# A convolution's product and gate turned by VectorE and DMA instead of TensorE, with the gate products moved to the end of the projection

## The chip, the cores and the metric

The kernel runs on one core of a Trainium2 chip. The metric is the device time of one execution, in microseconds. TensorE (PE) multiplies matrices, VectorE (DVE) and ScalarE (ACT) work on vectors, GpSimd (POOL) does small things, and SyncE (SP) issues most of the DMA transfers. Each engine works through its own list of instructions in order and waits for the others by semaphores.

## The reference

A decoder trunk of four layers over 256 tokens of 1024 numbers, all float32. Each layer adds half a SwiGLU feed-forward (2816 wide), then a mixer, then another half SwiGLU, each on an RMS-normalised x. The mixers by layer are: short gated convolution, latent attention, spatial gating, and short gated convolution again. The change touches the convolution (layers 0 and 3) and the spatial gating (layer 2):

```python
def short_conv_mixer(x, w_in, conv_k, w_out):
    proj = x @ w_in
    b_gate, c_gate, h = proj[..., :d], proj[..., d:2 * d], proj[..., 2 * d:]
    z = c_gate * h
    conv = lax.conv_general_dilated(z, conv_k[:, None, :], ...)   # 3 taps, causal, per channel
    return (b_gate * conv) @ w_out

def spatial_gating_mixer(x, w_in, v_norm, w_s, b_s, w_out):
    z = jax.nn.gelu(x @ w_in)
    u, v = z[..., :SG_WIDTH], z[..., SG_WIDTH:]
    v = rms_norm(v, v_norm)
    ...
    return (u * mixed.reshape(bsz, s, SG_WIDTH)) @ w_out
```

## The kernel before

**Products.** The 256 tokens are two tiles of 128, and each weight serves both. To keep float32 accuracy a weight is split into a rounded part `whi` (ScalarE, L106) and a remainder `wlo` (VectorE, L113), and the left operand likewise; a product is then three matmuls (L299, L300, L302): rounded by rounded, rounded by remainder, remainder by rounded. A unit of weights is 128 x 1024 numbers (two rows of the contraction at width 512), so a unit is six matmuls of 128 x 512. Units are split up to three ahead of their use, from six raw buffers that SyncE loads (L93), and nine buffers of split units go round.

**The order.** The order is written out by the program's own loop: two generators, one for each token tile, take turns, and one turn emits the products of one unit (six matmuls). The first tile runs four of its steps ahead. What is to follow a product some turns later is put in a list (`later(turns, ...)`) and emitted when its turn comes, on whatever engines it needs. A unit's remainder is emitted on VectorE at the start of the next turn.

**Turning.** A result has tokens on partitions; as the left operand of the next product it must have channels there. There are two ways. `transposed` lets TensorE transpose four 128 x 128 blocks into PSUM (L261). The other way is a VectorE transpose within blocks of 32 x 32, a DMA write of the half to DRAM and four DMA reads back that put the blocks in place; the feed-forward's hidden half takes this way always (`turned`), and x does in most places (`prepare_x`, L415 to L431), where SyncE's weight loads are held back from the write until the reads.

**The convolution block** (`conv`, lines 512 to 560). The projection makes c, h and b, each in two halves of 512 channels. A group of the first three products shares the first half of x, which is ready earlier (`linear_group`); in the kernel before these are c, h and b of half 0, and then c, h and b of half 1 follow. When an h is done, VectorE makes z = c*h (L548), two turns later TensorE transposes it, ScalarE copies it out of PSUM (L523), and VectorE applies three taps to each of four blocks (L528, L530). When a b is done ScalarE takes it out of PSUM (L553), TensorE transposes it, VectorE multiplies the gate (L537), and the result is split (L253, L254) as the left operand of the output product. The output product `rows_into_x` takes rows 0 to 3 (half 0) first and rows 4 to 7 (half 1) after.

**The spatial block** (`spatial`): v of both halves and u of half 0 in the group, then u of half 1. The product m = u * mixed (L639) is transposed by TensorE and split.

## Time and profile before

| what | value |
|---|---|
| median of 3 runs | 1857.88 us (1857.31 to 1858.77) |
| the profiled execution's own time | 1856.6 us |
| its span (first to last instruction) | 1854.9 us |
| TensorE busy | 1833.3 us, 99% |
| VectorE busy | 1119.6 us, 60% |
| ScalarE busy | 913.9 us, 49% |
| DMA | 400.26 MB, 216 GB/s on average |

Busy time of TensorE counts a stretch in which matmuls follow without a hole, so 99% says how seldom it waits and not how fast it works. A timeline row gives the start, the duration, the engine, the line, the operation, what it writes and reads, and in square brackets how long its engine was idle before it and who ended that.

### The profile page before, as it was taken

The numbers are of one execution on the slowest core, as the hardware profiler recorded it, in microseconds if no ns is written. First come the engines' busy times: TensorE is split into PE (matmuls) and PEld (weight loads), VectorE is DVE, ScalarE is ACT, GpSimd is POOL, SyncE is SP. The second block draws the span as 40 slices with busy tenths as digits, with TensorE's granted clock in tenths as the row PEclk, the third lists the DMA queues.
The fourth block names the chain that finished last, engine by engine and source line by source line (L and its number), as shares of the span: only waits on it lengthen the run. The fifth ranks groups of instructions, "written<-read, shape, count | busy, mean of one in ns | idle before, by whom it ended". The sixth has DMA issues, their size and how long they took to land.

```text
span 1854.9 us, 23375 instructions
## 1 busy us (share of the span) xinstructions
PE 1833.3 (99%) x8518; PEld 1506.0 (81%) x8518; DVE 1119.6 (60%) x1357; ACT 913.9 (49%) x1300; POOL 103.9 (6%) x222
## 2 busy tenths in 40 slices
PE   8999999999999989999999999999999999999999
PEld 6888878888888878888888888888888888788887
DVE  5655676655665576666556555665645665775662
ACT  5443645443644376544454446554545454545451
POOL 1000000000501031000010001000000000000000
PEclk9999999999999999999999999999999999999999
DMA  7776657776777550687777766577857785657782
GB/s 265 241 240 218 209 179 216 240 241 210 235 244 238 193 160 15 201 259 232 221 238 256 228 220 216 175 232 234 264 185 243 242 261 178 213 181 235 233 269 75
DMA packets 228980, 400.26 MB, mean 216 GB/s; under 512 B 17126, under 2 KB 77696, under 8 KB 228864
## 3 DMA queue, kind: packets, MB, share of 16 engines
q1 hardware_dynamic: 227856, 397.08, 67.0%
q8 instruction: 66, 1.08, 0.2%
q0 software_dynamic: 608, 1.11, 0.2%
q10 hardware_dynamic: 400, 0.57, 0.1%
q14 instruction: 50, 0.41, 0.1%
HBM read 365.67 MB, written 33.03 MB: 215 GB/s over the span
## 4 chain that ended last, share of the span: by engine, by line
PE 96%; ACT 2%; DVE 2%; issue 0%; DMA 0%; DVEq 0%; ACTq 0%
PE acc L299 31%; PE acc L300 31%; PE acc L302 31%; PE tr L261 1%; PE acc L938 1%; PE acc L911 1%; ACT whi L106 1%; DVE wlo L113 0%; DVE s L530 0%; ACT s L836 0%; ACT s L253 0%; PE acc L620 0%; DMA s<-in_norm_g_dram 0%; ACT s L817 0%; ACT s L860 0%
## 5 line engine op out<-in xcount | busy, mean ns | idle before, releaser
L299 PE MATMUL acc<-whi,s 128*128 128x512 f32 (+1 forms) x2664 | 1025.2, 385 | 2.8 <-ACT whi L106 1.3
L300 PE MATMUL acc<-wlo,s 128*128 128x512 f32 (+1 forms) x2664 | 1019.8, 383 | 2.1 <-DVE wlo L113 2.1
L302 PE MATMUL acc<-whi,s 128*128 128x512 f32 (+1 forms) x2664 | 988.2, 383 | 0.0
L113 DVE TENSOR_TENSOR wlo<-raw,whi 128x1024 fp32r<-128x1024 f32 (+1 forms) x634 | 747.3, 1212 | 131.0 <-ACT whi L106 129.2
L106 ACT ACTIVATE whi<-raw 128x1024 fp32r<-128x1024 f32 (+1 forms) x634 | 636.6, 1047 | 138.9 <-PE acc L302 120.3
L299 PEld LDWEIGHTS acc<-whi,s 128*128 128x128 f32 x2664 | 500.9, 188 | 107.8 <-ACT whi L106 2.5
L300 PEld LDWEIGHTS acc<-wlo,s 128*128 128x128 f32 x2664 | 501.0, 188 | 106.0 <-DVE wlo L113 3.0
L302 PEld LDWEIGHTS acc<-whi,s 128*128 128x128 f32 x2664 | 500.7, 188 | 106.1 <-DVE s L254 0.7
L479 ACT ACTIVATE s<-acc,rstd 128x512 f32<-128x512 f32 (+1 forms) x96 | 62.6, 652 | 446.4 <-PE acc L302 440.4
L487 DVE SCALAR_TENSOR_TENSOR s<-acc,rstd,s 128x512 f32<-128x512 f32 (+1 forms) x96 | 67.7, 705 | 173.6 <-PE acc L302 171.8
L286 DVE TENSOR_TENSOR s<-big,s 128x512 fp32r<-128x512 f32 x96 | 61.8, 644 | 128.1 <-ACT s L285 127.9
L381 ACT ACTIVATE s<-x 128x512 bf16<-128x512 f32 x48 | 30.2, 630 | 163.6 <-DVE x L400 125.9
L254 DVE TENSOR_TENSOR s<-s,s 128x512 fp32r<-128x512 f32 (+1 forms) x58 | 39.9, 688 | 107.6 <-ACT s L253 107.6
L389 POOL TENSOR_TENSOR total<-ss,ss 128x1 f32<-128x1 f32 x26 | 14.8, 570 | 1417.1 <-ACT s L381 1417.1
L400 DVE SCALAR_TENSOR_TENSOR x<-acc,x 128x512 f32<-128x512 f32 x32 | 22.1, 692 | 117.3 <-PE acc L302 117.2
L285 ACT ACTIVATE s<-big 128x512 fp32r<-128x512 f32 x96 | 56.3, 586 | 22.1 <-DMA big<-turn 22.0
L489 DVE STREAM_TRANSPOSE big<-s 128x512 f32<-128x512 f32 (+1 forms) x96 | 64.1, 667 | 3.3
L253 ACT ACTIVATE s<-s 128x512 fp32r<-128x512 f32 (+1 forms) x58 | 36.5, 629 | 42.1 <-DVE s L537 21.6
L431 ACT ACTIVATE s<-s,columns 128x128 f32<-128x128 f32 x136 | 43.1, 388 | 1.9 <-DMA s<-xturn 1.7
L261 PE MATMUL tr<-ident,s 128*128 128x128 f32 (+1 forms) x222 | 33.3, 276 | 9.8 <-DVE s L781 5.1
L261 PEld LDWEIGHTS tr<-ident,s 128*128 128x128 f32 (+1 forms) x222 | 25.8, 138 | 17.9 <-DVE s L781 7.3
L415 DVE STREAM_TRANSPOSE s<-x 128x512 f32<-128x512 f32 x34 | 24.2, 711 | 1.2
(123 smaller groups left out, 410.6 us busy)
## 6 DMA issues: line engine op xcount, KB each, us to landing
raw<-in_ffn_gate_dram SPq DMA_DIRECT2D x176, 512.0 KB, 4.8
raw<-in_ffn_up_dram SPq DMA_DIRECT2D x176, 512.0 KB, 5.0
raw<-in_ffn_down_dram SPq DMA_DIRECT2D x176, 512.0 KB, 5.0
raw<-in_conv_w_in_dram SPq DMA_DIRECT2D x48, 512.0 KB, 4.7
turn<-big SPq DMA_DIRECT2D x32, 512.0 KB, 4.0
big<-turn SPq DMA_DIRECT2D x128, 128.0 KB, 4.4
xturn<-s SPq DMA_DIRECT2D x34, 256.0 KB, 4.2
s<-xturn SPq DMA_DIRECT2D x136, 64.0 KB, 2.0
```

Of the source, the lines that this page charges most:

```text
L106: nc.scalar.activation(hi, src, AF.Copy)
L113: self.nc.vector.tensor_tensor(out=lo, in0=src, in1=hi.bitcast(F32), op=ALU.subtract)
L261: nc.tensor.transpose(tr[: part.shape[-1], n, :], part, ident)
L285: nc.scalar.activation(hi.rearrange("p k (i b) -> p k i b", b=32), src, AF.Copy)
L286: nc.vector.tensor_tensor(out=lo.rearrange("p k (i b) -> p k i b", b=32), in0=src, in1=hi.bitcast(F32).rearrange("p k (i b) -> p k i b", b ...
L299: nc.tensor.matmul(ps, lhsT=ah[:, k, :], rhs=wh[:, wk, c], start=first, stop=False)
L300: nc.tensor.matmul(ps, lhsT=ah[:, k, :], rhs=wl[:, wk, c], start=False, stop=False)
L302: nc.tensor.matmul(ps, lhsT=al[:, k, :], rhs=wh[:, wk, c], start=False, stop=last)
L431: nc.scalar.activation(xg[:, k, :].rearrange("p (i b) -> p i b", b=32), y[:, :, k], AF.Copy, scale=g[:, k : k + 1])
L479: nc.scalar.activation(sg[n], ps[:, :w], AF.Silu, scale=r)
L487: nc.vector.scalar_tensor_tensor(out=h, in0=ps[:, :w], scalar=r, in1=sg[n], op0=ALU.mult, op1=ALU.mult)
L489: nc.vector.transpose(z[0][:, :, k0 : k0 + w // P].rearrange("p j k b -> p k j b"), h.rearrange("p (k j b) -> p k j b", j=4, b=32))
```

## The change

In the convolution block both z (c*h) and b now go the other way: `turn_half`, taken out of `prepare_x`, transposes in blocks on VectorE, writes, reads, and calls what follows eight turns later (`M_TAKE`). The taps read a copy that ScalarE makes in four pieces (L529); the gate multiplies what was read (L542). The order of the six products is changed to c0, h0, c1, then h1, b0, b1, so both gates come last, just ahead of the output product. In the spatial block the half 1 of m goes this way, and half 0 still through TensorE. The DRAM buffers for such turns become eight.

```diff
-X_TURN, X_WRITE, X_READ, X_TAKE = 2, 1, 3, 12
+X_TURN, X_WRITE, X_READ, X_TAKE, M_TAKE = 2, 1, 3, 12, 8
...
+    def turn_half(src, take, turns):
+
         z = slot([P, 4, 4, 32])
-        nc.vector.transpose(z.rearrange("p j k b -> p k j b"), x_half(t, h).rearrange("p (k j b) -> p k j b", j=4, b=32))
-        d = dram.tile([4, 32, 4, 4, 32], F32, tag="xturn", name=name("xturn"))
+        nc.vector.transpose(z.rearrange("p j k b -> p k j b"), src.rearrange("p (k j b) -> p k j b", j=4, b=32))
+        d = dram.tile([4, 32, 4, 4, 32], F32, tag="xturn", name=name("xturn"), bufs=8)
         y = slot([P, 4, 4, 32])
...
         later(X_WRITE, write)
         later(X_READ, read)
-        later(X_TAKE, take)
+        later(turns, lambda: take(y))
...
-        def convolved(j, z):
-            zp = transposed([z[:, k * P : (k + 1) * P] for k in range(4)])
+        def convolved(j, y):
...
-            nc.scalar.activation(zT[:, :, 2 : P + 2], zp, AF.Copy)
+            for k in range(4):
+                nc.scalar.activation(zT[:, k, 2 : P + 2].rearrange("p (i b) -> p i b", b=32), y[:, :, k], AF.Copy)
...
-        def gated(j, bs):
-            bT = transposed([bs[:, k * P : (k + 1) * P] for k in range(4)])
+        def gated(j, y):
             m = slot([P, 4, P])
-            nc.vector.tensor_tensor(out=m, in0=bT, in1=shared["cv", t, j], op=ALU.mult)
+            nc.vector.tensor_tensor(out=m.rearrange("p k (i b) -> p i k b", b=32), in0=y,
+                                    in1=shared["cv", t, j].rearrange("p k (i b) -> p i k b", b=32), op=ALU.mult)
...
-            later(3, lambda: convolved(j, z))
+            turn_half(z, lambda y: convolved(j, y), M_TAKE)
...
-            later(2, lambda: gated(j, bs))
-
-        yield from linear_group(t, a, 512, NK, [lambda ps, f=f: f(0, ps) for f in (c_done, h_done, b_done)])
-        for f in (c_done, h_done, b_done):
-            f(1, (yield from linear(t, a, 512, NK)))
+            turn_half(bs, lambda y: gated(j, y), M_TAKE)
+
+        yield from linear_group(t, a, 512, NK, [lambda ps: c_done(0, ps), lambda ps: h_done(0, ps), lambda ps: c_done(1, ps)])
+        for f, j in ((h_done, 1), (b_done, 0), (b_done, 1)):
+            f(j, (yield from linear(t, a, 512, NK)))
...
-            later(2, lambda: gated(j, m))
+            if j == 0:
+                later(2, lambda: gated_by_pe(j, m))
+            else:
+                turn_half(m, lambda y: gated(j, y), M_TAKE)
```

The lists of two engines change as follows in the first convolution block (layer 0). `wlo79` is the remainder of weight unit 79, `acc` a product's PSUM bank, `tr` a transposed one, `columns1` the taps, `raw` a weight buffer, `xturn` the DRAM buffer of a turn.

VectorE before, around the first gate: the last taps of the first tile, two splits, the gate (L537) and the remainder of its result, and the second tile's c*h (L548).

```order
L530 SCALAR_TENSOR_TENSOR s_232_1946<-s_231_1943,columns1_85,s_232_1946 128x128 x2
L113 TENSOR_TENSOR wlo79_1930<-raw79_1818,whi79_1929 128x1024
L113 TENSOR_TENSOR wlo80_1971<-raw80_1836,whi80_1970 128x1024
L537 TENSOR_TENSOR s_237_1995<-tr_236_1990,s_232_1946 128x512
L254 TENSOR_TENSOR s_239_1998<-s_237_1995,s_238_1997 128x512
L113 TENSOR_TENSOR wlo81_2003<-raw81_1854,whi81_2002 128x1024
L548 SCALAR_TENSOR_TENSOR s_241_2020<-acc_219_1785,rstd_217_1782,s_233_1968 128x512
```

VectorE in the changed kernel, around its first gate (L542): the taps that end here are the second tile's, of half 1.

```order
L536 SCALAR_TENSOR_TENSOR s_278_2281<-s_277_2275,columns1_85,s_278_2281 128x128 x2
L113 TENSOR_TENSOR wlo91_2267<-raw91_2125,whi91_2266 128x1024
L426 STREAM_TRANSPOSE s_280_2305<-s_279_2303 128x4x4x32
L542 TENSOR_TENSOR s_286_2309<-s_271_2209,s_246_2009 128x4x4x32
L254 TENSOR_TENSOR s_288_2312<-s_286_2309,s_287_2311 128x512
L426 STREAM_TRANSPOSE s_290_2327<-s_289_2325 128x4x4x32
L113 TENSOR_TENSOR wlo92_2317<-raw92_2143,whi92_2316 128x1024
```

The first gate has moved from unit 80 to unit 91. It now stands behind all four sets of taps and behind the block transpose of the second tile's gate half.

SyncE before, at the loads of the output weights:

```order
L93 DMA raw91_2124<-in_conv_w_out_dram 128x1024
L93 DMA raw92_2142<-in_conv_w_out_dram 128x1024
L93 DMA raw93_2160<-in_conv_w_out_dram 128x1024
L93 DMA raw94_2182<-in_conv_w_out_dram 128x2x512
L93 DMA raw95_2223<-in_conv_w_out_dram 128x2x512
```

SyncE in the changed kernel, at the same place: the write of the second tile's c*h half 1 (`xturn_261`), the write of the first tile's gate half 0 (`xturn_270`), then the reads of both.

```order
L93 DMA raw92_2143<-in_conv_w_out_dram 128x1024
L93 DMA raw93_2161<-in_conv_w_out_dram 128x1024
L432 DMA xturn_261_2173<-s_260_2171 128x512
L432 DMA xturn_270_2208<-s_269_2206 128x512
L436 DMA s_262_2174<-xturn_261_2173 32x4x128 x4
L436 DMA s_271_2209<-xturn_270_2208 32x4x128 x4
L93 DMA raw94_2237<-in_conv_w_out_dram 128x2x512
```

Two turns stand between the loads, and the second turn's write is queued ahead of the first turn's reads.

## Rows read from the trace of the kernel before

**Rows 1.** The page: busy time of each engine, and the chain by engine.

```profile
PE 1833.3 (99%) x8518; PEld 1506.0 (81%) x8518; DVE 1119.6 (60%) x1357; ACT 913.9 (49%) x1300; POOL 103.9 (6%) x222
...
PE 96%; ACT 2%; DVE 2%; issue 0%; DMA 0%; DVEq 0%; ACTq 0%
```

**Rows 2.** Timeline of TensorE, first convolution block, around a group of transposes.

```profile
218.83 0.39 PE L299 MATMUL acc<-whi,s 128*128 128x512 f32 x1
...
221.38 0.39 PE L302 MATMUL acc<-whi,s 128*128 128x512 f32 x1
221.61 0.60 PE L261 MATMUL tr<-ident,s 128*128 128x128 f32 x4
221.97 0.48 PE L299 MATMUL acc<-whi,s 128*128 128x512 f32 x1
222.28 0.40 PE L300 MATMUL acc<-wlo,s 128*128 128x512 f32 x1
```

**Rows 3.** Timeline of TensorE, the wait in the same block.

```profile
232.02 0.39 PE L302 MATMUL acc<-whi,s 128*128 128x512 f32 x1
233.33 0.66 PE L261 MATMUL tr<-ident,s 128*128 128x128 f32 x4 [0.92 <-DVE s L548]
```

**Rows 4.** Timeline of VectorE, the same block; the last row is x's block transpose.

```profile
219.11 0.75 DVE L548 SCALAR_TENSOR_TENSOR s<-acc,rstd,s 128x512 f32<-128x512 f32 x1
219.78 1.22 DVE L113 TENSOR_TENSOR wlo<-raw,whi 128x1024 fp32r<-128x1024 f32 x1
...
222.88 0.29 DVE L528 TENSOR_SCALAR s<-s,columns 128x128 f32<-128x128 f32 x1 [1.87 <-ACT s L523]
...
226.78 2.35 DVE L113 TENSOR_TENSOR wlo<-raw,whi 128x1024 fp32r<-128x1024 f32 x2
229.05 0.68 DVE L537 TENSOR_TENSOR s<-tr,s 128x512 f32<-128x512 f32 x1
230.44 0.69 DVE L254 TENSOR_TENSOR s<-s,s 128x512 fp32r<-128x512 f32 x1 [0.70 <-ACT s L253]
...
232.52 0.75 DVE L548 SCALAR_TENSOR_TENSOR s<-acc,rstd,s 128x512 f32<-128x512 f32 x1
...
286.17 0.71 DVE L415 STREAM_TRANSPOSE s<-x 128x512 f32<-128x512 f32 x1
```

**Rows 5.** Timeline of ScalarE, the same block.

```profile
214.08 1.27 ACT L431 ACTIVATE s<-s,columns 128x128 f32<-128x128 f32 x4
...
225.24 0.68 ACT L553 ACTIVATE s<-acc,rstd 128x512 f32<-128x512 f32 x1
229.77 0.64 ACT L253 ACTIVATE s<-s 128x512 fp32r<-128x512 f32 x1 [3.85 <-DVE s L537]
```

**Rows 6.** The page's DMA issues of x's turns (median us to landing).

```profile
xturn<-s SPq DMA_DIRECT2D x34, 256.0 KB, 4.2
s<-xturn SPq DMA_DIRECT2D x136, 64.0 KB, 2.0
```

**Rows 7.** Waits of SyncE's queue: total us, times, longest.

```profile
SPq L425 <- DMA xturn<-s: 126.7, 34, 6.1
```

**Rows 8.** Timeline of SyncE's queue: four reads of a turn.

```profile
208.49 1.75 SPq L425 DMA_DIRECT2D s<-xturn  x4
```

**Rows 9.** Waits of TensorE: total us, times, longest; the longest of all.

```profile
PE tr L261 <- DVE s L781: 5.1, 6, 2.2
```

**Rows 10.** Timeline of TensorE, attention block.

```profile
678.47 0.79 PE L299 MATMUL acc<-whi,s 128*128 128x512 f32 x1 [1.31 <-ACT s L253]
```

**Rows 11.** Stretches in the attention block: busy us by engine, granted clock, DMA share, GB/s.

```profile
672.00:680.00 8.00, 5.41 (x24) 3.76 (x23) 6.43 (x18) 6.95 (x18) 4.39 (x7) 0.87 0.55 177
680.00:684.00 4.00, 3.93 (x20) 3.43 (x18) 2.91 (x13) 3.94 (x9) 3.51 (x5) 0.84 0.10 39
```

**Rows 12.** Timeline of ScalarE, spatial block: u evicted.

```profile
1173.66 0.69 ACT L634 ACTIVATE s<-acc,rstd 128x512 f32<-128x512 f32 x1 [0.66 <-PE acc L302]
```

**Rows 13.** Timeline of VectorE, spatial block: u multiplied.

```profile
1174.38 0.69 DVE L639 TENSOR_TENSOR s<-s,s 128x512 f32<-128x512 f32 x1 [1.43 <-ACT s L634]
```

More of the change, by code (lines that the diff above doesn't have):

```diff
@@ L413, in prepare_x, with take @@
             return
+        def take(y):
+            xg = slot([P, 4, P])
+            for k in range(4):
+                nc.scalar.activation(xg[:, k, :].rearrange("p (i b) -> p i b", b=32), y[:, :, k], AF.Copy, scale=g[:, k : k + 1])
+            lhs[t][h] = split(xg, [P, 4, P])
+        turn_half(x_half(t, h), take, X_TAKE)
+    def turn_half(src, take, turns):
         z = slot([P, 4, 4, 32])
-        nc.vector.transpose(z.rearrange("p j k b -> p k j b"), x_half(t, h).rearrange("p (k j b) -> p k j b", j=4, b=32))
-        d = dram.tile([4, 32, 4, 4, 32], F32, tag="xturn", name=name("xturn"))
+        nc.vector.transpose(z.rearrange("p j k b -> p k j b"), src.rearrange("p (k j b) -> p k j b", j=4, b=32))
+        d = dram.tile([4, 32, 4, 4, 32], F32, tag="xturn", name=name("xturn"), bufs=8)
         y = slot([P, 4, 4, 32])
@@ L426, in read @@
             W.hold(-1)
-        def take():
-            xg = slot([P, 4, P])
-            for k in range(4):
-                nc.scalar.activation(xg[:, k, :].rearrange("p (i b) -> p i b", b=32), y[:, :, k], AF.Copy, scale=g[:, k : k + 1])
-            lhs[t][h] = split(xg, [P, 4, P])
         later(X_WRITE, write)
         later(X_READ, read)
-        later(X_TAKE, take)
+        later(turns, lambda: take(y))
     def turn_by_pe(t, h, g):
@@ L506, in plan_conv @@
     def plan_conv(ia):
-        plan_group([(conv_w_in[ia], part * D) for part in (1, 2, 0)], 512, NK)
-        for part in (1, 2, 0):
-            W.add(conv_w_in[ia], part * D + 512, 512, NK, 2)
+        w = conv_w_in[ia]
+        plan_group([(w, D), (w, 2 * D), (w, D + 512)], 512, NK)
+        for c in (2 * D + 512, 0, 512):
+            W.add(w, c, 512, NK, 2)
         plan_rows(conv_w_out[ia], NK, OUT_TAIL)
@@ L522, in convolved @@
                 nc.vector.tensor_copy(out=zT[:, :, 0:2], in_=shared["z", t - 1, j][:, :, P : P + 2])
-            nc.scalar.activation(zT[:, :, 2 : P + 2], zp, AF.Copy)
+            for k in range(4):
+                nc.scalar.activation(zT[:, k, 2 : P + 2].rearrange("p (i b) -> p i b", b=32), y[:, :, k], AF.Copy)
             shared["z", t, j] = zT
@@ L625, in mix, with gated @@
             mixed[j] = mx
-        def gated(j, m):
-            ms[j] = lhs_of(m, 4)
+        def gated(j, y):
+            src = y.rearrange("p i k b -> p k i b")
+            hi, lo = slot([P, 4, P], F32R), slot([P, 4, P], F32R)
+            nc.scalar.activation(hi.rearrange("p k (i b) -> p k i b", b=32), src, AF.Copy)
+            nc.vector.tensor_tensor(out=lo.rearrange("p k (i b) -> p k i b", b=32), in0=src,
+                                    in1=hi.bitcast(F32).rearrange("p k (i b) -> p k i b", b=32), op=ALU.subtract)
+            ms[j] = hi, lo
         us = [None] * 2
@@ L639, in u_mixed, with gated_by_pe @@
             nc.vector.tensor_tensor(out=m, in0=us[j], in1=mixed[j].rearrange("p k n -> p (k n)"), op=ALU.mult)
-            later(2, lambda: gated(j, m))
+            if j == 0:
+                later(2, lambda: gated_by_pe(j, m))
+            else:
+                turn_half(m, lambda y: gated(j, y), M_TAKE)
+        def gated_by_pe(j, m):
+            ms[j] = lhs_of(m, 4)
         yield from linear_group(t, a, 512, NK, [v_done, v_done, lambda ps: u_done(0, ps)])
```

## The prediction, on record before the changed kernel was timed

> **What bounds the kernel now.** I read the page first: TensorE is busy 99% of the span and holds 96% of the chain that ended last [rows 1]. So only two things can move the time: what TensorE executes, and what it has to wait for. Then the timeline of TensorE through the first convolution block. Its products start 0.232 us apart (eleven starts from 218.83 to 221.38), so six of them, the share of one turn, take 1.39 us [rows 2]. A group of four transposes pushes this aside: without it the product after the one at 221.38 would start at 221.61 and the one after that at 221.84; they start at 221.97 and 222.28. A group costs 2.28 - 1.84 = 0.44 us. And there is one real stop per convolution block: after the product at 232.02 the next start is due at 232.25 and comes at 233.33, 1.08 us late, put down to VectorE [rows 3]. VectorE's own timeline tells why: the product c*h, which the transposes wait for, starts only at 232.52 because two weight splits, a gate and its split stand ahead of it in order [rows 4]. So VectorE is behind TensorE in this block although it is far from full over the span (60%). That is the state into which the change puts more VectorE work.
>
> **What goes.** 16 groups of four transposes in two convolution blocks and two in the spatial block, 18 x 0.44 = 7.9 us, all on the path, since TensorE has no other slack. The two stops of 1.08 us go too: nothing on TensorE waits for c*h any more. A convolution block gains 8 x 0.44 + 1.08 = 4.6 us, the spatial block 0.9 us; together 10.1 us.
>
> **What comes.** Per turned half: one VectorE transpose (0.71 us, the form of L415), one write of 256 KB and four reads of 64 KB on SyncE's queue, and for the convolved half four ScalarE copies (1.27 us like L431) in place of one eviction [rows 4, 5]. ScalarE is 49% busy and has room; those copies are priced at nothing but for their place in the chain below. The holds keep weight loads back for two turns, 2.8 us; six raw buffers are in hand, so I price that at nothing too (if that cover went, weight splits would come late, the third rival).
>
> What decides is the gates. They are now the last product but one and the last, and the output product follows them. From the end of the first h half of tile 0 (0 us here, 218.83 in the trace: the c*h at 219.11 starts 0.28 after it, [rows 2, 4]) to the first output product of tile 0 the order holds 29 turns (15 steps of each tile, one short), so the output product is due at 29 x 1.39 = 40.3 us. When is its left operand there? I walk VectorE's order of the changed kernel with the trace's spacings: c*h 0.67 (219.11 to 219.78), a weight split 1.17 (two in 2.35), the twelve taps of a half 3.9 (222.88 to 226.78), a transpose 0.64 (0.71 less the overlap of 0.07 that c*h shows) [rows 4].
> - The second tile's first h half ends at turn 7, 9.7 us; VectorE takes it at 10.0. From here its order has no hole: two c*h halves more (three in all), four transposes, three sets of taps and six weight splits up to the transpose of tile 0's first gate half: 3 x 0.67 + 4 x 0.64 + 3 x 3.9 + 6 x 1.17 + 0.3 for the small copies = 23.6, so it ends at 33.6 us, though TensorE delivered that gate half at 27.8.
> - SyncE has the write of that gate half queued ahead of the reads of the second tile's second c*h half. These reads start at 33.6 + 0.35 = 33.95, take 1.3 us to the last issue and land 2.0 us later: 37.3 us [rows 6, 8]. The write of that c*h half was issued at about 29; writes land in 4.2 us at the median and the 34 waits for one average 3.7, the longest 6.1 [rows 7], so the reads may start as late as 35.1 and land at 38.5.
> - Then in order: the first ScalarE copy 0.4, taps 3.9, one weight split 1.17, the transpose of tile 1's gate half 0.64, the gate multiply 0.68, ScalarE's rounding 0.64 with a hop of 0.05 [rows 4, 5]. From 37.3 that is 44.8, from 38.5 it is 46.0.
> - Bound from below: with the reads on time VectorE itself, after three weight splits, can begin these taps at 37.15 without the copy: 44.2 us.
>
> So TensorE stands still for 3.9 to 5.7 us; I take 5.0. Behind the waiting gate on VectorE stand the next transpose and the weight splits, but their units are three steps ahead of TensorE, and TensorE stands too.
>
> Tile 0's second gate half: its eviction stands on ScalarE behind that late rounding, so its transpose ends at 47.1, its write lands at 51.4, its reads at 54.7; and VectorE has the transpose of tile 1's second gate half ahead of the multiply, which TensorE delivers only two turns (2.8 us) before the product in need: hop 0.28, eviction 0.68, transpose 0.71, multiply 0.68, rounding 0.69 make 3.04 [rows 4, 5]. Late by 0.3 for the rounded part and 0.5 with the remainder. I take 0.5, and 1.7 as the upper end if the DMA is as late as its slowest wait. Tile 1's halves profit from the stops of tile 0 and come in time.
>
> The clock: TensorE's waits in this trace are at most 2.2 us long [rows 9], so a stop of 5 us has no row. The nearest: around a wait of 1.31 us in the attention block, the last of several, the granted clock fell from 2.4 to 1.2 GHz, 0.87 and 0.84 of full in two stretches of 8 and 4 us [rows 10, 11]. That is (0.13 x 8 + 0.16 x 4) / 0.5 = 3.4 us at half speed, 1.7 us lost. The wait of 2.2 us came later in that block without such a fall. So 0 to 1.7 per block; I take the middle, 0.8. The Trainium skill (TensorE: Matmul & The Clock Gate, "Why this matters for your kernels") says that idle gaps between bursts of matmuls put the clock back; the first of these rows agrees. By that rule alone both blocks would pay the 1.7 us.
>
> Spatial block: the second u half of tile 0 is evicted at 1173.66, multiplied at 1174.38 [rows 12, 13]; transpose, write, reads and rounding (0.71 + 4.2 + 1.3 + 2.0 + 0.6) bring it to about 1183.9, and its output product is nine turns after that turn's end, at 1173.4 + 12.5 = 1185.9 or later (transposes and mixing products lie between). It fits even with a late write. Gain 0.9.
>
> **Sum.** Per convolution block -4.6 + 5.0 + 0.5 + 0.8 = +1.7 us; twice, +3.4; spatial -0.9. Net +2.5 on the profiled execution's 1856.6 us. The median of the runs shown is 1.3 us above that execution, so I forecast 1857.9 + 2.5 = 1860.4. The ends of the terms: -4.6 + 3.9 per block gives -2.3 in all, and -4.6 + 5.7 + 1.7 + 1.7 gives +8.1.
>
> The Trainium skill (VectorE: DVE Perf Modes, "Rules for kernel authors") would transpose 128x128 on TensorE where PSUM will do, and it has VectorE's transpose as one of 32x32 blocks only. It speaks against this change, for which the rows show 0.44 us of TensorE on one side and 0.71 us of VectorE plus some 7.5 us of DMA (4.2 + 1.3 + 2.0) on the other; by it the time would rise, as in the forecast.
>
> **Rivals.**
> - *The wait doesn't come, the transposes are simply gone.* For it: TensorE is the bound and the DMA turns of x and of the feed-forward hidden half hardly hold ScalarE up now. Against it: those are taken twelve turns after, these eight, and VectorE's order has no hole between 10 and 33 us. It would need some 4.5 us less VectorE work ahead of the gate than I count. Time 1857.9 - 10.1 = 1848; half of the wait gives about 1853.
> - *The waits cost more than the transposes did* (slower). One mechanism: the first gate's multiply behind the taps in VectorE's order, at its late end, with the DMA at its slowest and the clock down in both blocks: +8.1, 1866. With the second stop of 0.5 and no clock loss, gain and loss are equal at a first stop of 4.1 us in the block alone, and at 4.5 us once half of the spatial gain is set against it; from there on the time rises. My walk ends just beyond that point, which is why this and no change lie close together.
> - *Weight splits come late too.* The split of unit 88 ends at 34.6 and TensorE uses it at about 35.0 us. If VectorE is 1 us later than walked, each block stops there as well. But this stop moves the gate's due time by as much, so the sum stays; only further splits late at other places would add, 1 to 2 us a block: 1863.
>
> **How the numbers follow.** A measurement of this kernel can tell about 0.2%, 3.7 us, from no change. The forecast with its own range of 1856 to 1864 has 0.50; the first rival, with the half-way case, 0.22; the second 0.18; the third 0.10. Of the forecast's half, some 0.12 lies above 1861.6 and nearly nothing below 1854.2; of the third rival 0.06 above. Hence slower 0.18 + 0.12 + 0.06 = 0.36, faster 0.21 (a little of the half-way case stays inside), the same 0.43. The range of 8 in 10 takes in most of the first rival's half-way case and the second: 1850 to 1867.
>
> **What would show it.** In the profile after: the TensorE line for transposes at 150 instead of 222 from slots; one idle of 4 to 6 us a convolution block ahead of the first output product with SyncE's, ScalarE's or VectorE's gate named; VectorE busy without a hole for some 23 us before the first gate's transpose; in SyncE's queue a wait of the gate's write for its transpose; the granted clock below full right after. The prediction is wrong if these stops are under 2 us, or if TensorE waits at other places (weights, x) for more than 2 us a block.

## The result, and the profile after

The changed kernel takes 1871.86 us at the median of six runs (1869.78 to 1874.23), the kernel before 1858.33 us in as many beside them (1857.31 to 1860.62): a ratio of 1.0069, 95% interval [1.0056, 1.0082]. It is 13.5 us slower. The prediction was 1860.4 us with a range of 1850 to 1867, so the result lies outside it, on the side that had the chance 0.36.

The page of the changed kernel answers [rows 1], [rows 6]:

```profile
span 1872.5 us, 23444 instructions
...
PE 1836.9 (98%) x8446; PEld 1504.0 (80%) x8446; DVE 1131.0 (60%) x1375; ACT 914.4 (49%) x1324; POOL 103.3 (6%) x222
...
PE 91%; DMA 3%; DVE 3%; ACT 1%; issue 1%; SPq 0%; POOL 0%; DVEq 0%; ACTq 0%
PE acc L299 30%; PE acc L302 30%; PE acc L300 30%; DMA xturn<-s 2%; DVE wlo L113 1%; PE tr L261 1%; DMA raw<-in_conv_w_in_dram 1%; PE acc L955 1%; PE acc L928 1%; DMA raw<-in_conv_w_out_dram 0%; DMA s<-xturn 0%; ACT whi L106 0%; DMA raw<-in_ffn_gate_dram 0%; SPq L436 0%; ACT s L253 0%
...
xturn<-s SPq DMA_DIRECT2D x52, 256.0 KB, 4.2
s<-xturn SPq DMA_DIRECT2D x208, 64.0 KB, 2.0
```

72 TensorE instructions are gone (8518 to 8446: 18 groups of four), and yet TensorE is busy 3.6 us longer: a product at the lower clock takes longer, here and in the attention block, which the change doesn't touch and where the lower clock was granted for 13.7 us (before: 6.8). The chain of work that ended last now runs for 3% of the span through DMAs, mostly `xturn<-s`, the writes of the turns. The median write still lands in 4.2 us. The waits of TensorE (total us, times, longest) answer [rows 9]:

```profile
PE acc L299 <- ACT s L253: 15.2, 3, 7.4
PE acc L300 <- DVE wlo L113: 4.3, 6, 0.9
```

The longest wait was 2.2 us and is now 7.4 us. It stands ahead of the output product, as the timeline of TensorE shows in both convolution blocks (it answers [rows 3]):

```profile
255.04 0.40 PE L299 MATMUL acc<-whi,s 128*128 128x512 f32 x1
256.33 0.50 PE L300 MATMUL acc<-wlo,s 128*128 128x512 f32 x1 [0.89 <-DVE wlo L113]
...
261.54 0.40 PE L302 MATMUL acc<-whi,s 128*128 128x512 f32 x1
269.29 0.80 PE L299 MATMUL acc<-whi,s 128*128 128x512 f32 x1 [7.36 <-ACT s L253]
269.88 0.63 PE L300 MATMUL acc<-wlo,s 128*128 128x512 f32 x1
270.31 0.63 PE L299 MATMUL acc<-whi,s 128*128 128x512 f32 x1
...
1654.23 0.80 PE L299 MATMUL acc<-whi,s 128*128 128x512 f32 x1 [6.55 <-ACT s L253]
```

Three things cost time here. A remainder (`wlo`) is late by 1.06 us at 256.33. The first output product is due at 261.54 + 0.23 and starts at 269.29, 7.52 us late. And after it products start 0.43 us apart and not 0.23. The stretches (columns as in [rows 11]) say why: the granted clock is 0.57 on average in the 12 us after 264. It was 1.2 GHz for 10.24 us from 264.9, when TensorE had stood still for 3 us; of these 10.24 us it stood for the first 4.4 and worked for the rest.

```profile
264.00:276.00 12.00, 6.71 (x17) 5.29 (x18) 9.40 (x16) 4.99 (x6) 0.00 (x0) 0.57 0.75 240
276.00:312.00 36.00, 35.94 (x157) 28.33 (x156) 25.56 (x30) 20.37 (x32) 2.73 (x6) 1.00 0.63 203
```

Now back along the chain. VectorE's timeline, first block:

```profile
249.73 0.71 DVE L426 STREAM_TRANSPOSE s<-s 128x512 f32<-128x512 f32 x1
...
254.46 0.70 DVE L426 STREAM_TRANSPOSE s<-s 128x512 f32<-128x512 f32 x1
255.09 3.45 DVE L113 TENSOR_TENSOR wlo<-raw,whi 128x1024 fp32r<-128x1024 f32 x3
258.46 0.17 DVE L527 COPY s<-s 128x8 f32<-128x8 f32 x1
262.27 0.28 DVE L534 TENSOR_SCALAR s<-s,columns 128x128 f32<-128x128 f32 x1 [3.65 <-ACT s L529]
...
266.16 1.22 DVE L113 TENSOR_TENSOR wlo<-raw,whi 128x1024 fp32r<-128x1024 f32 x1
267.30 0.70 DVE L426 STREAM_TRANSPOSE s<-s 128x512 f32<-128x512 f32 x1
267.93 0.65 DVE L542 TENSOR_TENSOR s<-s,s 128x512 f32<-128x512 f32 x1
```

and SyncE's queue (its own instructions: start, time to issue all of them):

```profile
248.12 1.81 SPq L93 DMA_DIRECT2D raw<-in_conv_w_out_dram  x4
250.47 5.05 SPq L432 DMA_DIRECT2D xturn<-s  x2
258.31 3.64 SPq L436 DMA_DIRECT2D s<-xturn  x8
```

The second tile's z half 1 is transposed at 249.73 and its write issued at 250.47. Four loads that had been held back for the turn before stand right ahead of it. The last of them, issued at 249.50, takes 8.1 us and lands at 257.6; the write lands 0.7 us behind it, at 258.3, 7.8 us after its issue, and only then can the reads start. ScalarE:

```profile
261.93 0.91 ACT L529 ACTIVATE s<-s 128x128 f32<-128x128 f32 x4 [6.59 <-DMA s<-xturn]
...
268.61 0.63 ACT L253 ACTIVATE s<-s 128x512 fp32r<-128x512 f32 x1 [5.20 <-DVE s L542]
```

Its copies (L529) begin at 261.93, VectorE's taps at 262.27 after 3.65 us without work. Behind these taps, in VectorE's order, stand a weight split, a transpose, and the gate of the *first* tile's half 0. Its rounding (L253) ends at 268.61 + 0.63 = 269.24, and TensorE starts.

**The account.** Per block I summed, from each product's start to the next start on TensorE, what exceeds 0.232 us (1585 to 1700 for the second block, 200 to 312 for the first). Steps over 0.5 us are stops. Smaller ones while the granted clock is 1.2 GHz are products at that clock; steps of 0.1 to 0.5 us over at the full clock are small late starts. The transposes count whole. In us:

| kernel, block | transposes and small | remainder late | wait for operand | small late starts | at 1.2 GHz | sum | against before |
|---|---|---|---|---|---|---|---|
| before, 1 | 4.6 | – | 1.08 (L548) | – | – | 5.7 | |
| before, 2 | 4.4 | – | 1.10 (L548) | – | – | 5.5 | |
| after, 1 | 1.2 | 1.06 | 7.52 | 0.9 | 2.8 | 13.4 | +7.7 |
| after, 2 | 1.2 | 1.62 | 6.71 | 0.7 | 1.6 | 11.8 | +6.4 |

The 1.62 us are two stops of 0.55 and 1.06. Of the small late starts, 0.52 and 0.50 us are one further wait in two steps, for the first tile's second gate half, at 283.37 and 284.09 in the first block; the rest (0.3 and 0.2) is around the late remainders. PEld is TensorE's load of the left operand:

```profile
283.37 0.19 PEld L299 LDWEIGHTS acc<-whi,s 128*128 128x128 f32 x1 [0.42 <-ACT s L253]
284.09 0.19 PEld L302 LDWEIGHTS acc<-whi,s 128*128 128x128 f32 x1 [0.43 <-DVE s L254]
```

Together the blocks are +14.1 us, as much as the medians differ (13.5). The two profiled executions differ by 17.6 us; most of what is left of that lies at the start (1.2 us) and in attention (1.4 us), which the change doesn't touch and which differ between executions (next section).

### The profile page after: what moved, and what is told of

Read it like the earlier page. It is cut to its first block, busy times and chain, and to the rows that moved or that the text cites. A ratio compares the mean times of both kernels' runs of the same rounds, so it can differ in the third digit from the quotient of the medians.

```text
span 1872.5 us, 23444 instructions
## 1 busy us (share of the span) xinstructions
PE 1836.9 (98%) x8446; PEld 1504.0 (80%) x8446; DVE 1131.0 (60%) x1375; ACT 914.4 (49%) x1324; POOL 103.3 (6%) x222
## 3 DMA queue, kind: packets, MB, share of 16 engines
q8 instruction: 66, 1.08, 0.2%
## 4 chain that ended last, share of the span: by engine, by line
PE 91%; DMA 3%; DVE 3%; ACT 1%; issue 1%; SPq 0%; POOL 0%; DVEq 0%; ACTq 0%
PE acc L299 30%; PE acc L302 30%; PE acc L300 30%; DMA xturn<-s 2%; DVE wlo L113 1%; PE tr L261 1%; DMA raw<-in_conv_w_in_dram 1%; PE acc L955 1%; PE acc L928 1%; DMA raw<-in_conv_w_out_dram 0%; DMA s<-xturn 0%; ACT whi L106 0%; DMA raw<-in_ffn_gate_dram 0%; SPq L436 0%; ACT s L253 0%
## 5 line engine op out<-in xcount | busy, mean ns | idle before, releaser
L253 ACT ACTIVATE s<-s 128x512 fp32r<-128x512 f32 (+1 forms) x58 | 36.4, 628 | 41.0 <-DVE s L542 20.4
L261 PE MATMUL tr<-ident,s 128*128 128x128 f32 (+1 forms) x150 | 24.0, 289 | 6.2 <-DVE s L798 3.3
L261 PEld LDWEIGHTS tr<-ident,s 128*128 128x128 f32 (+1 forms) x150 | 18.0, 142 | 11.6 <-DVE s L798 5.4
```

Source lines behind the costliest of these rows:

```text
L261: nc.tensor.transpose(tr[: part.shape[-1], n, :], part, ident)
```

## The experiments

Three theories at first. *Q*: SyncE's queue makes the trip of the convolved half long, because its write follows a bunch of held-back loads. *V*: VectorE's own list is too long, whatever the trip takes. *G*: the new order of the products, with both gates last, is at fault by itself. Each experiment is told with its time, its ratio to the kernel before on the same chip, and then the same account.

**The kernel before, once more.** 

> The kernel before itself, profiled once more, for what changes from one execution to the next. In the changed kernel's trace the first weight's rounding comes 1.2 us later than in the trace of before, and TensorE has 13.7 us at the lower clock in the attention block against 6.8. If these belong to the execution: both differ here from the first trace of before too. If they belong to the change (a program with more instructions): they are as in the first trace, within 0.3 us and 3.4 us.


It took 1858.32 us, span 1856.6. Its first remainder comes 0.7 us later than in the first trace of before, its 21st 1.7 us later, and the distance stays 1.7 us to the end. So a start that is 1 to 2 us longer belongs to the execution. In attention the lower clock was granted for 3.4 us here, for 6.8 in the first trace and 13.7 in the trace after, so that varies with the execution too. Attention took between 0 and 2 us longer than in the first trace in kernels that don't touch it. Of traces only the account of the blocks is compared.

**Gates by TensorE, z by DMA.** 

> As the changed kernel, but the convolution's gate halves are transposed by TensorE again (two turns after their product); the product c*h still goes by VectorE and DMA, and the order of products stays c0, h0, c1, h1, b0, b1. Theory Q (SyncE's queue: a turn's write stands behind weight loads that were held back and let go together, so what is read back is late, and the first gate stands in VectorE's list behind taps that wait for it): the first gate's multiply moves ahead of the taps that wait for the late read, so the stops of 7.4 and 6.6 us before the first output product are gone. 8 groups of product transposes and 2 spatial ones at 0.44 us and the two old stops of 1.08 us are saved: 4.4 + 2.2 = 6.6 us under the kernel before, 1851 to 1853. Theory V (VectorE's list alone is full in this block, whatever the DMA does): the taps, splits and block transposes of c*h stay, so a stop of 2 to 4 us a block remains: 1856 to 1860. Theory G (the gates come last, and that alone makes their result late): stops of some 5 us a block remain: 1860 to 1865.

```diff
         def gated(j, y):
             m = slot([P, 4, P])
-            nc.vector.tensor_tensor(out=m..., in0=y, in1=shared["cv", t, j]..., op=ALU.mult)
+            bT = transposed([y[:, k * P : (k + 1) * P] for k in range(4)])
+            nc.vector.tensor_tensor(out=m, in0=bT, in1=shared["cv", t, j], op=ALU.mult)
...
-            turn_half(bs, lambda y: gated(j, y), M_TAKE)
+            later(2, lambda: gated(j, bs))
```

1863.21 us, 1.0022 [1.0013, 1.0032]: 8.7 us of the loss are gone, but it is no gain. The time lies in G's range, but without G's stop: in place of the operand's stop TensorE waits for a gate's eviction, 2.40 us in the first block and 2.77 in the second, and there for a remainder too, 2.19 us. In the first block that eviction stands on ScalarE behind the copies of a z that is read back late:

```profile
250.54 0.91 ACT L529 ACTIVATE s<-s 128x128 f32<-128x128 f32 x4 [5.30 <-DMA s<-xturn]
...
252.30 0.67 ACT L559 ACTIVATE s<-acc,rstd 128x512 f32<-128x512 f32 x1
```

**z by TensorE, gates by DMA.** 

> As the changed kernel, but the product c*h is transposed by TensorE as in the kernel before; only the gate halves (and the spatial half) go by VectorE and DMA, gates last. Q: SyncE has one turn at a time in its queue, the gate's write is no longer queued with that of c*h, and no taps wait for a read; from the end of the gate's product 0.3 + 0.7 + 0.7 + 4.2 to 6 + 1.3 + 2.0 + 0.7 + 0.7 = 10.6 to 12.4 us to the rounded gate against the 12.5 us of nine turns: stops of 0 to 1 us. 10 groups at 0.44 = 4.4 saved, the old stop of 1.08 stays: 1854 to 1857. V: VectorE has lost two block transposes a tile and block, stops of 2 to 3 us: 1858 to 1862. G: the stops stay at 5 to 7 us a block: 1866 to 1872.

```diff
-            turn_half(z, lambda y: convolved(j, y), M_TAKE)
+            later(3, lambda: convolved(j, z))
```

1861.21 us, 1.0014 [1.0004, 1.0023]. With z off the trip the first operand is in time, and the later ones are late by 1.9 and 2.2 us (block 1) and 2.2 us (block 2). In block 1 the second tile's first gate half is read back late, and the gate after it stands behind that one in VectorE's list:

```profile
272.67 0.69 DVE L542 TENSOR_TENSOR s<-s,s 128x512 f32<-128x512 f32 x1 [4.72 <-DMA s<-xturn]
```

The time and the size of the stops are what V expected, but the wait in block 1 is ended by a read. So neither half of the convolution's change pays by itself.

**The turns on GpSimd's queue.** 

> As the changed kernel, but the writes and reads of the eight-turn turns are issued from GpSimd's queue, which is idle there, and weight loads on SyncE's queue are not held back for them. VectorE's list is the same. Q: a write no longer stands behind four weight loads (it took 7.8 us from issue to the reads in the changed kernel), so it lands in 4 to 5 us and the stop before the first output product shrinks by 2.5 to 4 us a block, and so does the clock's loss: 1861 to 1867. V and G: VectorE's order and the place of the gates are the same, the stops stay at 6.5 to 7.5 us: 1870 to 1873.

```diff
-            nc.sync.dma_start(out=d..., in_=z)
+            eng.dma_start(out=d..., in_=z)      # nc.gpsimd for the new turns, no hold of the loads
```

1891.64 us, 1.0175 [1.0160, 1.0191], much worse. The DMA view gives the issues of these turns:

```profile
xturn<-s POOLq DMA_DIRECT2D x18, 256.0 KB, 3.7
s<-xturn POOLq DMA_DIRECT2D x72, 64.0 KB, 5.2
```

Against [rows 6] the writes are shorter (3.7 for 4.2 us) and the reads, with loads in flight beside them, 5.2 us for 2.0. Another queue didn't free these transfers from the traffic; Q's forecast of 1861 to 1867 failed here. The kernel changes two things, the queue and the hold; the run without the hold on SyncE's queue (below) has the hold alone.

**The order alone.** 

> As the kernel before in how everything is transposed (TensorE for c*h, gates and both spatial halves); of the change only the order of the projection's products is kept: c0, h0, c1, h1, b0, b1. Theory G (gates last is itself what makes them late): a stop of 2 to 7 us a block before the first output product, 1862 to 1871. Theories Q and V (the trip by VectorE and DMA makes them late, the order only removes the cover): no new stop of note, 1856 to 1860.

```diff
-        yield from linear_group(t, a, 512, NK, [... c, h, b of half 0])      # then c, h, b of half 1
+        yield from linear_group(t, a, 512, NK, [c of half 0, h of half 0, c of half 1])
+        for f, j in ((h_done, 1), (b_done, 0), (b_done, 1)):
```

All transposes by TensorE. 1856.03 us, 0.9989 [0.9979, 0.9998]: G falls. The account has no stop at all in either block (sums 4.3 and 4.5 us for 5.7 and 5.5); TensorE is busy without a hole:

```profile
215.00:312.00 97.00, 97.00 (x442) 78.99 (x441) 69.41 (x110) 51.91 (x76) 2.74 (x6) 1.00 0.62 203
1585.00:1700.00 115.00, 115.00 (x518) 93.42 (x517) 79.46 (x121) 58.74 (x84) 2.75 (x6) 1.00 0.63 205
```

**No trip at all.** 

> As the changed kernel, but the eight-turn turns leave out the write to DRAM and the reads: what follows reads VectorE's block transpose directly (blocks are not put in place). All VectorE and ScalarE instructions and their order stay. This is the bound of VectorE's list with a DMA of no time. Q: the stop before the first output product falls from 7.4 and 6.6 us to the 3.9 us that VectorE's list was walked to, or less, the late remainders of weights (1.06 us a block) stay: 1857 to 1863. V: the stops stay at 6 to 7 us: 1869 to 1872. If DMA were everything, the full 10 us would be gained: 1848.

```diff
+        if turns == M_TAKE and trip[0] is False:
+            later(turns, lambda: take(z))
+            return
```

1863.01 us, 1.0025 [1.0015, 1.0034]. VectorE's list alone stops TensorE for 4.05 and 3.97 us; the walk's lower bound was 3.9. (Its lines are numbered one higher.)

```profile
264.87 0.50 PE L300 MATMUL acc<-whi,s 128*128 128x512 f32 x1 [3.88 <-ACT s L254]
```

So V holds for the floor: even a free trip would have lost.

**Loads not held back.** 

> As the changed kernel, but weight loads are not held back between the write and the reads of the eight-turn turns (still for x). In the changed kernel the writes that had four loads let go just ahead of them took 6.0 and 7.8 us to the reads. Theory Q with the bunch as its cause: loads spread out, a write has one or two loads ahead and lands in 4 to 5.5 us, but a read has loads ahead too; with turns from GpSimd's queue without a hold the reads took 5.2 us instead of 2.0. If the bunch is the larger part: stops 1 to 2 us shorter, 1867 to 1870. If a load ahead costs a read as much as a write: the same trip or a longer one, stops of 7 to 10 us, 1872 to 1885.

```diff
-            W.hold(1)
+            W.hold(int(turns != M_TAKE))
...
-            W.hold(-1)
+            W.hold(-int(turns != M_TAKE))
```

1877.59 us, 1.0102 [1.0087, 1.0117], 5.7 us worse than the changed kernel. From 225 to 262 us its four writes land in 4.7 us at the median (after: 5.9), its twenty reads in 3.4 (after: 2.0). By the account its two blocks are 4.8 us longer than those of the changed kernel: 2.9 us are remainders that come later still (2.7 and 2.9 us for 1.06 and 1.62), 1.4 us the stops (7.95 and 7.71 us). So the hold is worth more than its bunches cost the writes. That the longer reads make the remainders late, through the taps in front of them, is my reading and not tested apart.

**z taken twelve turns later, gates by TensorE.** 

> As the run with the gates by TensorE (c*h by VectorE and DMA), but what is read back of c*h is taken twelve turns after instead of eight. In that run TensorE stopped 2.2 and 2.6 us for ScalarE, which stood at a copy of c*h whose reads had not landed, with a gate's eviction queued behind it. Theory Q: with four turns (5.6 us) more the reads have landed when ScalarE comes to them, these stops go, and of the 6.6 us saved on TensorE most is seen: 1851 to 1855, faster than the kernel before. Theory V: the same VectorE work comes later, nearer to the output product, and remainders of weights or gates are late there: 1857 to 1862.

```diff
-            turn_half(z, lambda y: convolved(j, y), M_TAKE)
+            turn_half(z, lambda y: convolved(j, y), 12)
```

1863.67 us, 1.0030 [1.0019, 1.0041]: no better than with eight turns. Q falls; V's reason is what is seen, 1.7 us above V's range. The wait for the eviction is gone, and a remainder is late instead, by 3.39 and 3.40 us, because the taps come later and three weight splits stand behind them (VectorE):

```profile
268.29 0.29 DVE L534 TENSOR_SCALAR s<-s,columns 128x128 f32<-128x128 f32 x1 [0.37 <-ACT s L529]
...
272.18 3.49 DVE L113 TENSOR_TENSOR wlo<-raw,whi 128x1024 fp32r<-128x1024 f32 x3
```

**Only half 0, or only half 1, without its trip.** 

> The changed kernel in which z of half 0 alone does not go to DRAM and back: ScalarE takes VectorE's block transpose directly (the placing of the blocks is left out for that half). VectorE's and ScalarE's lists stay as they are; z of half 1, both gates and the spatial half make their trip. In the changed kernel the write of the second tile's z half 1 (7.8 us) was issued behind four weight loads let go after the reads of half 0. Queue theory: those four loads go earlier, the write lands in 4 to 5 us, VectorE's list alone decides and the stop ahead of the output product falls from 7.5 and 6.7 to about 4 to 5: 1864-1867. Rival (the reads, the taps or the gate's own trip set the stop, or the write is slow whatever stands ahead of it): write still 6 to 8 us, stops of 6.5 to 7.5, 1870-1873.

> The mirror of it: z of half 1 alone does not go to DRAM (its block placing left out); half 0, both gates and the spatial half make their trip. Queue theory: the late operand was z of half 1, so the taps start early and the stops fall to the 3.9 to 4.2 us that VectorE's list takes by itself: 1863-1866. Rival (the gates' own trip is as late as the taps): stops of 6 us and more, 1869-1873.

```diff
-            turn_half(z, lambda y: convolved(j, y), M_TAKE)
+            turn_half(z, lambda y: convolved(j, y), M_TAKE, j != 0)      # j != 1 in the second
```

Without half 0's trip 1867.20 us, 1.0046 [1.0032, 1.0060], stops of 5.79 and 5.07 us; without half 1's 1864.90 us, 1.0036 [1.0023, 1.0050], stops of 4.06 and 3.98 us. The second settles which operand is late: with z half 1 there, the stop is the floor, though half 0 and all gates still travel.

```profile
262.05 0.40 PE L302 MATMUL acc<-whi,s 128*128 128x512 f32 x1
266.34 0.50 PE L299 MATMUL acc<-whi,s 128*128 128x512 f32 x1 [3.90 <-ACT s L253]
```

The first is less clear than hoped: in it too four loads stood ahead of the write (issued at 244.77, the write at 248.79), which took 6.3 us. Its write landed 0.9 us behind the last of these loads. It gains 1.7 us of stop, but can't tell the loads from the trip.

**The order with the spatial half by DMA.** 

> The new order of the six products with all of the convolution's transposes on TensorE (1856.0 by itself), and the spatial half 1 by VectorE and DMA as in the changed kernel. By the prediction's term the spatial half gives 2 x 0.44 = 0.9 us: 1855; by the changed kernel's trace 0.3 to 0.5 us: 1855.6. Rival (its trip delays weights beside it): 1857-1858, no faster than the order alone.

```diff
-                later(2, lambda: gated_by_pe(j, m))
+                turn_half(m, lambda y: gated(j, y), M_TAKE)
```

1855.81 us (11 runs, 1853.31 to 1856.95), 0.9985 [0.9976, 0.9994]; the convolution blocks again without a stop. This is the fastest kernel here, 2.5 us below before. What the spatial half adds to the order alone (0.2 us) can't be told from nothing, so the times neither show nor refute the forecast of 0.9. The traces, one execution of each, speak for it: from the block's first group of transposes to x's first one 24.89 us pass (1167.11 to 1192.00) for 25.73 in the order alone (1168.45 to 1194.18), 0.84 us less.

**And z of half 0 by DMA too.** 

> The same, and z of half 0 by VectorE and DMA too: this operand has the product of c half 1, h half 1 and both gates' products ahead of its use, so its trip should cost nothing, and four groups of transposes of 0.44 us leave TensorE in the two convolution blocks: 1.8 us less than the one without, 1853.5-1854.5. Rival (VectorE's two transposes more per block, and held loads let go in bunches, make remainders late at the block's end): a stop of 1 to 3 us per block, 1856-1861.

```diff
-            later(3, lambda: convolved(j, z))
+            if j == 0:
+                turn_half(z, lambda y: convolved(j, z, y), M_TAKE)
+            else:
+                later(3, lambda: convolved(j, z))
```

1863.49 us, 1.0027 [1.0016, 1.0039]. My expectation failed, though this operand had far more time than any other. VectorE and TensorE:

```profile
240.29 0.29 DVE L538 TENSOR_SCALAR s<-s,columns 128x128 f32<-128x128 f32 x1 [1.06 <-ACT s L533]
...
248.29 3.49 DVE L113 TENSOR_TENSOR wlo<-raw,whi 128x1024 fp32r<-128x1024 f32 x3
```
```profile
246.36 0.40 PE L299 MATMUL acc<-whi,s 128*128 128x512 f32 x1
249.56 0.80 PE L300 MATMUL acc<-wlo,s 128*128 128x512 f32 x1 [2.81 <-DVE wlo L113]
```

Taken later, half 0's taps fall together with half 1's: 8.0 us of taps in a row (240.29 to 248.29), and the remainder behind them is 2.97 us late (3.17 in the second block). Two groups of transposes a block, 0.9 us, don't pay for that.

**Loads behind the write; loads held through the trip.** These two ask why the decisive write took 7.8 us. 

> The changed kernel with one difference: the four weight loads that were let go ahead of the write of the second tile's z half 1 are let go right behind that write; its reads are not covered by a hold. In the changed kernel this write took 7.8 us and the stop was 7.5 us. Theory that the loads ahead in the queue make the write long: it lands in 2 to 4 us (writes with no load in the 6 us before them landed in 2.0 us); the reads, which stand behind the first gate's write in SyncE's queue and could start at 255.5 at the earliest instead of 258.3, then have loads in flight beside them and take 3 to 5 us instead of 2; the stop is 4.5 to 6.5 us, 1866-1871. Rival (the write shares the DMA engines with whatever is in flight and is as long with loads behind it): still 6 to 8 us, a stop of 7.5 us or more, 1872-1876.

> The changed kernel with the loads held back through the whole of that trip: from the write of the first tile's z half 1 until the reads of the second tile's z half 1 are issued. No weight load is then in flight beside the trip. Theory of traffic: write 2 to 3 us, reads 2 us, starting when the first gate's write is issued (255.5), so the operand comes some 2.8 us sooner and VectorE's list decides: stop of 4 to 5.5 us if the weights are not late. But the loads come 10 us later: with six raw buffers and three units split ahead the remainders of the output product can be late by 1 to 5 us (a wait at a remainder in place of the old one); 1866-1872. Rival (the trip is long by itself, without loads): write still 6 us and more, stop of 7 us.

```diff
         def write():
-            W.hold(1)
+            W.hold(holds[0][0])
             nc.sync.dma_start(out=d..., in_=z)
+            W.hold(holds[0][1])
...
-            W.hold(-1)
+            W.hold(holds[1])
...
+            # (hold before, hold after the write), at the reads; for z half 1 of the first tile ((1, 0), 0),
+            # of the second ((0, -1), 0) in the one kernel and ((1, 0), -2) in the other
```

Loads behind the write: 1873.45 us, 1.0073 [1.0056, 1.0090], as slow as the changed kernel. SyncE's queue:

```profile
249.80 0.34 SPq L432 DMA_DIRECT2D xturn<-s  x1
250.24 3.07 SPq L93 DMA_DIRECT2D raw<-in_conv_w_out_dram  x4
254.52 0.33 SPq L432 DMA_DIRECT2D xturn<-s  x1
254.94 8.18 SPq L437 DMA_DIRECT2D s<-xturn  x8
```

The write lands in 3.2 us for 7.8 (second block: 2.2 for 7.3), with nothing changed but the loads' place: ahead of it they had made it long. The reads start 5.1 us after the write's issue (after: 7.8), right behind the first gate's write, which stands ahead of them in the queue; but they take 4.9 to 6.6 us to land (after: 1.9 to 2.8), with the loads now in flight beside them. ScalarE's copies begin 12.4 us after the write's issue (262.16; after: 11.5) and the stops are 8.42 and 6.26 us. In the first block nothing is won; the delay has moved from the write to the reads. The theory was right on the write and wrong on the sum.

Loads held through the trip: 1879.87 us, 1.0113 [1.0098, 1.0128], worse. The write takes 4.1 us (second block: 2.0), the reads 2.1 to 2.5, so z half 1 has arrived by 258.3. But ScalarE waits 10.35 us for the weights that were held, and VectorE's list for it, with the taps behind the split:

```profile
262.32 1.06 ACT L106 ACTIVATE whi<-raw 128x1024 fp32r<-128x1024 f32 x1 [10.35 <-DMA raw<-in_conv_w_out_dram]
```
```profile
263.41 1.23 DVE L113 TENSOR_TENSOR wlo<-raw,whi 128x1024 fp32r<-128x1024 f32 x1 [7.23 <-ACT whi L106]
...
265.04 0.29 DVE L535 TENSOR_SCALAR s<-s,columns 128x128 f32<-128x128 f32 x1 [0.32 <-ACT s L530]
```

The stop is 11.52 and 10.93 us. The middle of my own expectation (4 to 5.5 us if the weights are in time) fails on its condition; that the trip is long by itself falls too. Why 4.1 us in the first block, with no other transfer of the kernel in flight? The DMA view of 249.2 to 253.5 has, besides the write's 144 packets (q1), one packet of 16 KB of an instruction queue (q8):

```profile
q8 instruction: 1, 0.02, 2.3%
```

It took 1.60 us (250.30 to 251.90). 135 of the write's packets had started by 250.9, the other nine one after another from 251.89 on; so these probably stood behind it on one DMA engine. In all runs together 120 writes on SyncE's queue found no transfer of the kernel in flight; the 96 with no instruction packet of 8 or 16 KB beside them landed in at most 2.2 us, and all that took longer had one.

No run here has the write and the reads short and the weights in time as well, so what the trip would then cost beyond VectorE's 4.0 us isn't shown.

## Why the prediction was wrong

**Right.** The place and the shape: one stop ahead of the first output product, VectorE's order with the taps in front of the first gate, a rounding (L253) as the releaser, the clock below full after it. Also that the order holds no slack: the floor by VectorE alone was walked as 3.9 us and measured as 4.0 to 4.1 in the two kernels that take the late trip away. And the transposes are worth what [rows 2] said: transposes and small steps fall by 3.5 and 3.2 us a block, for 8 x 0.44 = 3.5, and the two old stops of 1.1 us went. The second stop was right too: walked as 0.5 us for the first tile's second gate half (0.3 for the rounded part, the rest for the remainder), with the transpose of the second tile's half ahead of the multiply, and measured as 0.52 and 0.50 us, in steps of about 0.26 for each part.

**The step that failed first** is the stop: "So TensorE stands still for 3.9 to 5.7 us; I take 5.0." It measured 7.52 and 6.71. The term in it that was mis-sized is the write of the second tile's z half 1: "so the reads may start as late as 35.1", from a longest wait of 6.1 us among 34 [rows 7]. On the same scale (the first h half of tile 0 ends at 220.02 in the trace after) the write was issued at 30.45, for "about 29", and the reads started at 38.3. I had drawn a write's time from the median and the longest wait over the program, in places where the order was made for it. Here it is the transfer right after another turn, and the loads that this turn held back go ahead of it. The rest of the chain held: from the landing of the reads (261.91) to the end of the rounding 7.3 us, walked as 7.5. A smaller slip stands ahead of it: VectorE's order was to have no hole, and it waited 1.14 us for the copy of the second tile's z half 0, itself read back late, which is most of the 1.5 us by which the write of half 1 came later than walked:

```profile
241.65 0.29 DVE L534 TENSOR_SCALAR s<-s,columns 128x128 f32<-128x128 f32 x1 [1.14 <-ACT s L529]
```

**Behind that lies an assumption:** "six raw buffers are in hand, so I price that at nothing too". The weights' loads and the trips share one stock of DMA time, and it has none to spare just here (DMA share 0.94 from 250.0 to 253.6 us, 0.99 from there to 256.4). Three kernels give the loads another place: ahead of the write (after: write 7.8, reads 2.0), behind it (write 3.2, reads 4.9 to 6.6), behind the reads (write 4.1, reads 2.1 to 2.5, but ScalarE 10 us without weights). The stop was 7.5, 8.4 and 11.5 us. The prediction's rule of looking where a hidden thing costs when its cover goes was stated and not carried through: the third rival counted late splits only.

**The clock** was put at 0.8 us a block and took 2.8 and 1.6. Its bound of 1.7 came from one stop of 1.31 us [rows 10, 11]; the trace of before has another stretch at 1.2 GHz at 712.0, behind waits of about 1 us, which the prediction did not use. TensorE was at 1.2 GHz for 10.24 us after 264.9 and 6.83 us after 1650.7, partly while it stood and partly while it worked. After stops of 4 us (without the trip, or without half 1's) 1.6, 2.7, 1.6 and 1.6 us were lost, some 1.8 in the mean. By this alone the walked +1.7 a block would have been +2.7.

**The remainders** came 1.06 and 1.62 us late, as the third rival had it ("1 to 2 us a block"). Its argument that such a stop moves the gate's due time by as much, so that the sum stays, holds in the first block: the write that decided was issued at 250.47, before the remainder's stop at 256.33. Without that stop the wait for the operand would have been longer by it. On the prediction's own scale the operand was ready at 49.2 (269.24), 8.9 us after the due time of 40.3, for the 3.9 to 5.7 that were walked.

Put together, per block: predicted -4.6 + 5.0 + 0.5 + 0.8 = +1.7; measured -4.5 + 7.52 (stop) + 1.06 + 0.3 (remainders) + 0.5 (second stop) + 2.8 (clock) = +7.7 and -4.3 + 6.71 + 1.62 + 0.2 + 0.5 + 1.6 = +6.4. Of the miss of 5.3 us a block on average, 2.1 us are the stop, 1.6 us the remainders, 1.4 us the clock, and 0.2 us a smaller gain. The spatial block's 0.9 us measured 0.4 in the trace after and 0.8 where it was changed beside the order alone, and isn't resolved by the medians.

## What to carry to other kernels

Where one engine is 99% busy, taking 0.44 us off it is worth 0.44 us only if no in-order list that feeds it gets longer at the same place; walk that list first, and take the price of a DMA from the transfers that stand where the new one will stand, not from the median over the program. Here the trace of before would have given it: 23 of its 27 writes that were issued behind weight loads still in flight landed 0.5 to 0.8 us after the last of these loads, so the place of the loads sets the write. A write and read back through DRAM beside a stream of weights isn't free even when every buffer seems to be in hand: try where the displaced loads go. And when such a change bundles an order with new transfers, time the order by itself: here it was the part that gained.

## What the hardware showed that I had not expected

- A write of 256 KB on one queue took from 2.0 us (seven writes with no weight load in flight, 2.0 to 2.4) to 7.8 us. What sorts it is the loads of 512 KB that are still in flight when it is issued: with one, two, three or four the means are 3.2, 4.3, 5.4 and 6.9 us (6, 22, 13 and 4 writes of the changed kernel), and 37 of these 45 writes landed 0.5 to 0.8 us after the last of the loads. The Trainium skill (DMA: Bandwidth & Descriptors, "Anatomy of one DMA") fits a DMA issued from GpSimd at about 2.0 us plus its bytes over 436 GB/s; by it 256 KB would take an estimated 2.6 us. The writes without traffic agree roughly; the others are up to three times that.
- Reads with loads in flight took 5.2 us at the median on GpSimd's queue and 3.4 us on SyncE's (225 to 262 us), for 2.0 us on SyncE's with the loads held back: the hold makes them short, and GpSimd's queue did not.
- A write with no other transfer of the kernel in flight, but one instruction packet of 16 KB beside it, took 4.1 us for the 2.0 us of the same write in the other block.
- A stop of 7.5 us cost 2.8 us more at the lower clock behind it, stops of 4 us 1.6 to 2.7 us, and stops of 3.0 and 3.2 us (z of half 0 by DMA) 2.1 us and nothing, so this price scatters.
